# The last feed-forward of a two-layer backbone as seven-product tiles, with sums of weight halves made by accumulating transfers

## The chip, the cores and the metric

The kernel runs on one core of one Trainium2 chip. The metric is the device time of one execution in microseconds (us). The work is shared by TensorE (PE, with its weight loads as PEld), VectorE (DVE), ScalarE (ACT), GpSimd (POOL) and SyncE (SP), which issues the loads.

## The reference

Two layers work on 512 latent tokens and 256 context tokens of width 1024. Each layer is a half-step SwiGLU feed-forward, a mixing of three head groups (grouped-query attention, a gated short convolution, a low-rank attention), and a second half-step feed-forward. Each sub-layer's input is normed and modulated.

```
def rms_norm(x, g):
    y = xf * lax.rsqrt(jnp.mean(xf * xf, axis=-1, keepdims=True) + EPS)
def modulate(h, shift, scale):
    return h * (1 + scale) + shift
def swiglu(h, wg, wu, wd):
    return (jax.nn.silu(h @ wg) * (h @ wu)) @ wd
def half_ffn(h, g, shift, scale, gate, wg, wu, wd):
    return h + 0.5 * gate * swiglu(modulate(rms_norm(h, g), shift, scale), wg, wu, wd)
```

The hidden width of a feed-forward is 2816, which is 22 tiles of 128. Shift, scale and gate are products of nine 1024 x 1024 blocks per layer with silu(c). The output is the latent stream alone, so the last feed-forward (layer 1, the second one) works on the 512 latent tokens only; the other three work on all 768.

## The kernel before, in words

Everything is kept transposed: features on the 128 partitions, tokens along the free dimension. The residual stream is eight tiles xT0 to xT7. A float32 product is made as three fp32r products: operands are split into a high half (a cast on ACT, tiles wh, s and the like) and a low half (raw minus high on DVE, wl), and hi·hi, hi·lo and lo·hi are summed in PSUM (tiles ps and po). So each weight block is loaded by SP, cast by ACT, subtracted by DVE, and then used by TensorE. Weight blocks of 512 KB use the tag wr, which has two buffers (NWR).

Each engine runs its instructions in program order, which the kernel's text fixes: chain and unchain keep the written order on TensorE, DVE and ACT. Every engine call goes through one helper (line 66), so most rows of the profile carry L66 and are told apart by tile names.

`ffn` computes a feed-forward in chunks of hidden tiles. For each hidden tile it makes the gate and the up product, SiLU and their product; after a chunk, a down pass multiplies the chunk's activations by the down weights for the eight outputs and adds gate times the result to xT. A *classical* tile makes both products with full width: 8 k-blocks x 3 products x 2 (gate, up), 48 matmuls of 512 columns when only the latents are there. The three joint feed-forwards (768 tokens) do their first chunk or two like this and then use *seven-product tiles* (class Tile): the tokens and the model width are halved, and seven products of sums of halves replace eight products of halves. The sums of the hidden state are made once (`sums`, `sums_late`); the sums of the weights are made per tile (class Weights: u up weights, g gate weights, s sums). A tile's products p1, p2, p6, p5, p7, p3, p4 are 12 matmuls each, of 384 columns with 768 tokens. While TensorE computes tile m, SP loads the gate and up weights of m+1, DVE forms the sums and ACT and DVE split the four parts: gate (w1), sum (w2), up (w3) and the fourth sum (w4). The joint chunks have three such tiles, then the down pass. The last feed-forward was classical throughout, in chunks of 8, 7 and 7.

`residual` is the last down pass of a sub-layer. It also computes the next sub-layer's norm: squares of xT are summed by products with ones, mean and rsqrt follow on DVE (tiles m), and the result is spread by transposes (R1 for the second token stream). E holds the next sub-layer's first weights; the third pair is split within its loop over k. `pump` does pieces of modulation in between: a piece loads 512 KB (tag mr) and DVE multiplies and sums it by scalar_tensor_tensor into junk, once for latents and once for context. The number npump says how many pieces follow each output; `pump(upto=...)` finishes what a gate needs.

`mixing` projects, norms and attends. Before the attention's units, the norm of the low-rank q (cq) and of k, v (ckv) are counted by products with ones (count_steps), and `uq` makes the q up projections. `wn_late` brings natural-layout weights one k block at a time.

Of the kernel before, what the change touches and what calls it, by code (L numbers as in the profile page):

```python
# [24 lines left out]
CHUNKS = ((0, 8), (8, 7), (15, 7))  # L25
# [17 lines left out]
LATE = {k: 1 for k in range(8)}  # L43
# [4 lines left out]
def tile_net(ctx: ExitStack, tc: tile.TileContext, a, out):  # L48
# [373 lines left out]
    def residual(blocks, rhs, gate, streams, nxt, pre=None, late={}, view=nv, npump=0, ntail=3):  # L422
# [3 lines left out]
        g = mod[gate]  # L426
# [90 lines left out]
        run(4)  # L517
# [27 lines left out]

        for k in range(KD + 1):
# [51 lines left out]
    def ffn(l, f, hin, streams, nxt, pre, npump, late={}):  # L598
# [5 lines left out]
        fast = w == T  # L604
        view = tv if fast else nv
        res = None

        def classical(m, ahead):
# [14 lines left out]
            else:  # L623
                pts = [ps(), ps()]
                for j in range(2):
                    project(full(pts[j]) if fast else plain(pts[j], cols), wgu[j], h)
                parts = [(banks(pts[0]), banks(pts[1]), pairs) if fast else
# [20 lines left out]
        if not fast:  # L648
            for ci, (m0, n) in enumerate(CHUNKS):
                acts = []  # L650
                for m in range(m0, m0 + n):
                    acts.append(classical(m, {}))
                    if m < 18:
                        pump(npump)
                if ci == 0:
                    pump(upto=gate)
                lastc = ci == len(CHUNKS) - 1
                if lastc:
                    before_last()
                res = residual(down(m0, n), acts, gate, streams, nxt if lastc else None, pre, late if lastc else {})  # L660
            return res


        nslow = 2 if i == 0 else 1
        U, V, t1 = [None] * 4, [None] * 2, [None] * 2

        def sums(j):

            X, Y = temp(), temp()
            lo, hi = slice(0, HALF), slice(HALF, T)  # L670
            c = slice(HALF * (j % 2), HALF * (j % 2) + HALF)
            if j % 2 == 0:
                t1[j // 2] = slot()
                V[j // 2] = slot(F32R), slot(F32R)
            T1, (vh, vl) = t1[j // 2][:, c], V[j // 2]
            ve.tensor_add(X, f32(h[j][0]), f32(h[j][1]))
            ve.tensor_add(Y, f32(h[j + 4][0]), f32(h[j + 4][1]))
            ve.tensor_sub(T1, X[:, hi], X[:, lo])
            ve.tensor_sub(X[:, lo], Y[:, hi], X[:, hi])
            ve.tensor_sub(Y[:, hi], Y[:, hi], T1)  # L680
            ve.tensor_sub(Y[:, lo], Y[:, lo], Y[:, hi])
            se.copy(vh[:, c], X[:, lo])
            ve.tensor_sub(vl[:, c], X[:, lo], f32(vh)[:, c])
            U[j] = slot(F32R), slot(F32R)
            se.copy(U[j][0], Y)
            ve.tensor_sub(U[j][1], Y, f32(U[j][0]))

        def sums_late():

            hi = slice(HALF, T)  # L690
            for j in range(4):
                T1 = t1[j // 2][:, HALF * (j % 2):HALF * (j % 2) + HALF]
                se.copy(h[j][0][:, hi], T1)
                ve.tensor_sub(h[j][1][:, hi], T1, f32(h[j][0])[:, hi])

        chunks = FIRST if i == 0 else FAST
        sums_at = (2, 3, 4, 5) if i == 0 else (0, 1, 2)
        for ci in range(nslow):
# [16 lines left out]
            residual(down(m0, n), acts, gate, streams, None, view=tv)  # L715
        W = {}

        class Weights:


            def __init__(self, m):
                self.m = m

# [21 lines left out]
            def fourth(self):  # L745
                ve.tensor_sub(self.g[:, 512:1024], self.g[:, 512:1024], self.s[:, 512:1024])
# [4 lines left out]
            def split_fourth(self):  # L751
                t = pool.tile([P, 1024], F32R, name=nm("w4"), tag="mr", bufs=2)
# [4 lines left out]
        b11 = [tuple(t[:, 0:HALF] for t in h[k]) for k in range(4)]  # L757
        s1 = [tuple(t[:, HALF:T] for t in h[k]) for k in range(4)]
        b21 = [tuple(t[:, 0:HALF] for t in h[k + 4]) for k in range(4)]
        b22 = [tuple(t[:, HALF:T] for t in h[k + 4]) for k in range(4)]  # L760

        def seventh(out, wb, at, mv, new, end=True):

            wh, wl = wb
            for k in range(4):
                c = slice(at + k * P, at + (k + 1) * P)
                for p, (st, m) in enumerate(((wh, mv[k][0]), (wh, mv[k][1]), (wl, mv[k][0]))):
                    te.matmul(out=out[:, 0:HALF], lhsT=st[:, c], rhs=m, start=new and k == 0 and p == 0,
                              stop=k == 3 and p == 2, skip_group_check=True)

        lo, hi = slice(0, HALF), slice(HALF, T)
# [1217 lines left out]
```

## Time and profile before

| | us |
|---|---|
| median of 3 runs | 2800.01 (2799.33 to 2801.71) |
| the profiled execution's own time | 2797.64 |
| its span | 2795.8 |
| TensorE busy | 2696.0 (96%) |
| VectorE busy | 1944.1 (70%) |
| ScalarE busy | 1089.0 (39%) |
| GpSimd busy | 146.9 (5%) |

The shares are means over the whole span. A timeline row gives the start, the length, the engine, the line, the operation with its output, its input and its shape, and in brackets how long the engine stood idle before it and what ended that. The last feed-forward runs from 2421 us to the end.

### The profile page before, as it was taken

What the parts mean: (1) busy time and instruction counts of PE and PEld (TensorE: products, weight loads), DVE (VectorE), ACT (ScalarE), POOL (GpSimd) and SP (SyncE); (2) the same over time, 40 slices, a digit from 0 to 9 for tenths busy, and PEclk for the clock granted to TensorE, in tenths of its full rate; (3) what the DMA queues carried; (4) which work ended last, traced back from release to release, by engine and by line L of the source; (5) the groups of instructions that cost most, each with busy time, mean ns of one, the idle gap of its engine ahead of it and who ended that gap; (6) DMA issues with size and microseconds to landing.
All of it is one profiled execution on the core that took longest, in us unless ns stands there. A gap on an engine that the chain in (4) does not pass through costs nothing. (4 is left out here: it accounts for less than half of the span.)

```text
span 2795.8 us, 38908 instructions
## 1 busy us (share of the span) xinstructions
PE 2696.0 (96%) x15440; PEld 2515.6 (90%) x15440; DVE 1944.1 (70%) x3293; ACT 1089.0 (39%) x1860; POOL 146.9 (5%) x194
## 2 busy tenths in 40 slices
PE   8999999999889998999999999999999999999999
PEld 5999999988788888999999899999988788888887
DVE  6857777777688866777777777777766798633333
ACT  5223333341478532333334333333342477322221
POOL 0000000001132200000000000000000233000000
PEclk9999999999999999999999999999999999999999
DMA  7313333233000321333333133333225101232332
GB/s 245 121 56 103 106 106 106 83 103 115 29 2 9 106 77 53 98 106 107 107 107 102 50 94 107 109 107 108 86 64 172 32 9 56 90 104 91 91 98 91
DMA packets 95269, 251.80 MB, mean 90 GB/s; under 512 B 11376, under 2 KB 40816, under 8 KB 95088
## 3 DMA queue, kind: packets, MB, share of 16 engines
q1 hardware_dynamic: 95088, 249.33, 28.2%
q8 instruction: 121, 1.98, 0.3%
q14 instruction: 60, 0.49, 0.1%
HBM read 247.19 MB, written 2.10 MB: 89 GB/s over the span
## 5 line engine op out<-in xcount | busy, mean ns | idle before, releaser
L66 PE MATMUL ps<-s,wh 128*128 128x384 f32 (+2 forms) x4724 | 1146.5, 349 | 17.3 <-DVE xT L66 11.9
L66 PEld LDWEIGHTS ps<-s,wh 128*128 128x128 f32 x4724 | 832.7, 188 | 90.2 <-issue 15.1
L66 PE MATMUL ps<-s,wl 128*128 128x384 f32 (+2 forms) x2362 | 707.4, 347 | 0.3 <-DVE wl L66 0.3
L66 PE MATMUL po<-s,wh 128*128 128x384 f32 (+2 forms) x2476 | 643.7, 341 | 2.4 <-ACT t L66 1.7
L66 PEld LDWEIGHTS po<-s,wh 128*128 128x128 f32 x2476 | 447.0, 188 | 15.6 <-ACT t L66 2.7
L66 PEld LDWEIGHTS ps<-s,wl 128*128 128x128 f32 x2362 | 428.7, 188 | 32.7 <-DVE wl L66 0.8
L66 PE MATMUL po<-s,wl 128*128 128x384 f32 (+2 forms) x1238 | 422.2, 341 | 0.3 <-DVE wl L66 0.3
L66 ACT CAST wh<-wr 128x1024 fp32r<-128x1024 f32 (+5 forms) x219 | 209.1, 957 | 449.1 <-PE ps L66 319.1
L66 DVE TENSOR_TENSOR wl<-wr,wh 128x1024 fp32r<-128x1024 f32 (+5 forms) x219 | 243.3, 1113 | 194.1 <-ACT wh L66 191.8
L66 DVE SCALAR_TENSOR_TENSOR xT<-ps,mod,xT 128x256 f32<-128x256 f32 (+1 forms) x392 | 212.6, 585 | 193.8 <-PE ps L66 191.9
L66 DVE SCALAR_TENSOR_TENSOR junk<-mr,sb 128x1024 fp8e4<-128x1024 f32 x224 | 273.4, 1221 | 16.4 <-DMA mr<-in_wm_dram 15.5
L66 PEld LDWEIGHTS po<-s,wl 128*128 128x128 f32 x1238 | 232.2, 188 | 6.7 <-DVE wl L66 0.5
L66 PE MATMUL po<-s,s 128*128 128x256 f32 (+3 forms) x952 | 157.6, 316 | 9.6 <-DVE t L66 3.7
L66 PEld LDWEIGHTS po<-s,s 128*128 128x128 f32 x952 | 140.5, 190 | 17.7 <-ACT s L66 6.5
L66 ACT COPY t<-po 128x384 f32<-128x384 f32 (+1 forms) x161 | 76.9, 478 | 195.2 <-PE po L66 194.2
L66 ACT ACTIVATE t<-t 128x384 f32<-128x384 f32 x106 | 55.7, 526 | 238.2 <-DVE t L66 238.2
L66 DVE TENSOR_TENSOR t<-ps,t 128x384 f32<-128x384 f32 (+3 forms) x91 | 55.3, 608 | 112.3 <-PE ps L66 110.3
L66 DVE TENSOR_TENSOR s<-t,s 128x768 fp32r<-128x768 f32 (+2 forms) x129 | 98.6, 767 | 41.0 <-ACT s L66 40.8
L66 ACT CAST s<-t 128x768 fp32r<-128x768 f32 (+2 forms) x129 | 87.9, 684 | 97.2 <-DVE t L66 96.9
L66 PE MATMUL po<-s,w 128*128 128x384 f32 x636 | 119.7, 336 | 0.0
L66 PE MATMUL po<-ident,t 128*128 128x128 f32 x684 | 101.7, 280 | 13.9 <-ACT t L66 12.9
L66 DVE TENSOR_TENSOR t<-po,t 128x384 f32<-128x384 f32 (+2 forms) x169 | 94.0, 557 | 28.6 <-ACT t L66 28.0
(180 smaller groups left out, 3094.6 us busy)
## 6 DMA issues: line engine op xcount, KB each, us to landing
mr<-in_wm_dram SPq DMA_DIRECT2D x128, 512.0 KB, 3.7
wr<-in_wg_dram SPq DMA_DIRECT2D x88, 512.0 KB, 3.5
wu<-in_wu_dram SPq DMA_DIRECT2D x53, 512.0 KB, 3.6
t<-in_wd_dram SPq DMA_DIRECT2D x56, 384.0 KB, 3.4
wr<-in_wu_dram SPq DMA_DIRECT2D x35, 512.0 KB, 3.5
wr<-in_wiT_dram SPq DMA_DIRECT2D x22, 512.0 KB, 3.5
wr<-in_wd_dram SPq DMA_DIRECT2D x16, 512.0 KB, 3.5
wr<-in_wo_dram SPq DMA_DIRECT2D x14, 512.0 KB, 4.0
```

The source lines that it names most:

```text
L66: f(*args, **kw)
```

## The change

The diff makes five changes.

1. *Last feed-forward.* Four classical tiles, then 18 seven-product tiles in chunks of six (LAST), with 256 columns per product. The class Weights gets a second way: SP loads u, and POOL issues three more transfers, a copy of u's first half into s (L751), u's second half added to it (L752), and the gate's first half added onto u (L753). DVE makes one sum of 512 columns (s + g). The fourth sum is an accumulating transfer too (L783: s added onto g's second half). To make all of them additions, the up part is computed negative, and the gate factor `minus` is the negated one. Weights are fetched two tiles ahead. Down weights come one output at a time.
2. *residual.* The third pair of E is split at k 4 and 5 instead of 6; the second stream's counts, mean and rsqrt come one step earlier, ahead of the products.
3. *wn_late.* Two k blocks per load, four loads of 768 columns for eight of 384.
4. *mixing, before the attention.* The rsqrt of ckv stands behind the query splits, a dummy Exp makes ACT load its table earlier, and the counts of cq go from the first up projection into the second, their mean into attention unit 1.
5. *mixing's residual.* npump is 2 instead of 1.

The core of the diff:

```
+LAST = ((0, 4), (4, 6), (10, 6), (16, 6))
-LATE = {k: 1 for k in range(8)}
+LATE = {0: 1, 2: 1, 4: 1, 6: 1}
...
-        run(4)
+        run(8 if ntail == 6 else 4)
...
-            if k == 6 and len(E) == 2:
-                E.append(wsplit(raws[2], 1024))
+            if k == 4 and len(E) == 2:
+                third.extend(pool.tile([P, 1024], F32R, name=nm(t), tag=t, bufs=3) for t in ("wh", "wl"))
+                se.copy(third[0], raws[2])
             if prev is not None:
                 prev.low()
-                if k <= hold or k == KD:
-                    products(k - 1)
-            prev = cur
+            if k == 5 and third:
+                ve.tensor_sub(third[1], raws[2], f32(third[0]))
+                E.append(tuple(third))
             second_update()
             second_square()
             run(3)
-            if k == 2:
+            if k == 1:
                 S[1].zero()
                 S[1].count(S[1].acc, False)
-            if k >= 2:
-                for _ in range(2 if k < 7 else len(s1)):
+            if k >= 1:
+                for _ in range(2 if k < 6 else len(s1)):
...
-            if k == 7:
-
+            if k == 6:
                 S[1].mean()
                 r1 = rsqrt(S[1].ms, S[1].w // P)
+            if prev is not None and (k <= hold or k == KD):
+                products(k - 1)
+            prev = cur
+            if k == 7:
+
                 R1 = po()
...
             def __init__(self, m):
                 self.m = m
+                if not joint:
+
+                    self.u = pool.tile([P, 1024], F32, name=nm("wu"), tag=("mscr", "mq")[m % 2], bufs=1)
+                    self.s = pool.tile([P, 1024], F32, name=nm("ws"), tag="mr", bufs=2)
+                    g, u, lo, hi = a["wg"][i, m], a["wu"][i, m], slice(0, 512), slice(512, 1024)
+                    nc.sync.dma_start(out=self.u, in_=u)
+                    pe.dma_start(out=self.s[:, lo], in_=u[:, lo])
+                    pe.dma_start(out=self.s[:, lo], in_=u[:, hi], accum_op=ALU.add)
+                    pe.dma_start(out=self.u[:, lo], in_=g[:, lo], accum_op=ALU.add)
...
             def sums(self):
                 g, u = self.g, self.u
                 lo, hi = slice(0, 512), slice(512, 1024)
+                if not joint:
+                    ve.tensor_add(self.s[:, hi], self.s[:, lo], g[:, lo])
+                    return
...
             def fourth(self):
+                if not joint:
+                    pe.dma_start(out=self.g[:, 512:1024], in_=self.s[:, 512:1024], accum_op=ALU.add)
+                    return
...
             def split_fourth(self):
+                if not joint:
+                    self.w4 = slot(F32R)[:, 0:512], slot(F32R)[:, 0:512]
+                    se.copy(self.w4[0], self.g[:, 512:1024])
+                    ve.tensor_sub(self.w4[1], self.g[:, 512:1024], f32(self.w4[0]))
+                    return
...
+        def further(m):
+            if not joint and m < NFF:
+                fetch(m)
...
         def update(o, pt):
+            if not joint:
+                x = tv(xT[o], LAT)
+                ve.scalar_tensor_tensor(out=x, in0=cv(pt, LAT), scalar=minus[:, o:o + 1], in1=x, op0=ALU.mult, op1=ALU.add)
+                return
...
                     t.gate1()
+                    further(m + 2)
                     nx.split_gate()
...
-            elif i == 4:
-                rr["ckv"] = rsqrt(stats["ckv"].ms, NT)
...
         stats["cq"].accumulate()
+        se.activation(out=small(1), in_=zeros[:, 0:1], func=AF.Exp)
+        rr["ckv"] = rsqrt(stats["ckv"].ms, NT)
...
-        sums = uq(0, stats["cq"].count_steps(stats["cq"].acc))
-        stats["cq"].mean()
-        sums()
+        uq(0)()
...
-        up_at(0, uq, 1)
+        up_at(0, lambda t: uq(t, stats["cq"].count_steps(stats["cq"].acc)), 1)
         at(0, "end", lambda: uq(2)())
+        at(1, "b", lambda: stats["cq"].mean())
...
-        return residual(lambda o: first_out[0] if o == 0 else wblock(a["wo"][l, o]), rhs, (l, 5), streams, nxt, pre, npump=1)
+        return residual(lambda o: first_out[0] if o == 0 else wblock(a["wo"][l, o]), rhs, (l, 5), streams, nxt, pre, npump=2)
```

How the rows move on the engines. In the names, the number tells tiles of one name apart. First the last feed-forward. POOL's order in the changed kernel, two tiles (wu is u, wr is g, ws is s; POOL had no transfers before):

```order
L751 DMA ws_24392<-in_wu_dram 128x512
L752 DMA ws_24392<-in_wu_dram 128x512
L753 DMA wu_24391<-in_wg_dram 128x512
L783 DMA wr_24361<-ws_24295 128x512
L751 DMA ws_24521<-in_wu_dram 128x512
L752 DMA ws_24521<-in_wu_dram 128x512
L753 DMA wu_24520<-in_wg_dram 128x512
L783 DMA wr_24489<-ws_24392 128x512
```

Each tile is three transfers for the tile two ahead and one onto the gate buffer of the next tile, in one queue.

ACT in the last feed-forward, before (two weight blocks wh per classical tile, SiLU and the activation's split):

```order
L66 CAST wh_24279<-wr_24277 128x1024
L66 CAST wh_24285<-wr_24283 128x1024
L66 CAST wh_24348<-wr_24346 128x1024
L66 CAST wh_24354<-wr_24352 128x1024
L66 ACTIVATE t_24339<-ps_24289 128x512
L66 CAST wh_24417<-wr_24415 128x1024
L66 CAST s_24342<-t_24339 128x512
```

and one tile of the changed kernel (t are gate and up parts from PSUM, wr the gate, ws the sum, wu the up part, s_23606 the fourth part, s_23631 the activation):

```order
L66 COPY t_23483<-po_23484 128x256
L66 ACTIVATE t_23483<-t_23483 128x256
L66 COPY t_23483<-po_23484 128x256
L66 CAST wh_23556<-wr_23505 128x1024
L66 COPY t_23585<-po_23484 128x256
L66 CAST wh_23588<-ws_23408 128x1024
L66 ACTIVATE t_23358<-t_23358 128x256
L66 CAST s_23606<-wr_23377 128x512
L66 CAST wh_23627<-wu_23407 128x1024
L66 CAST s_23631<-t_23358 128x512
```

There are ten rows to a tile instead of four; the split of the gate just loaded (wr_23505) and of its sum (ws_23408) stands ahead of the split of the fourth part out of the gate buffer of the tile at work (wr_23377).

Second, TensorE before the attention of layer 1. Before (ident are transposes, ones the counts of cq, we the first up projection):

```order
L66 MATMUL po_19970<-ident,s_19244 128x128
L66 MATMUL po_19975<-ident,s_19558 128x128
L66 MATMUL po_19975<-ident,s_19595 128x128
L66 MATMUL po_20005<-zeros,ident 128x8
L66 MATMUL po_20005<-ones,s_19849 128x2
L66 MATMUL ps_20004<-we_19938,s_19845 128x288
L66 MATMUL ps_20004<-we_19939,s_19845 128x288
L66 MATMUL ps_20004<-we_19938,s_19846 128x288
```

and the changed kernel at the same place, and some rows on:

```order
L66 MATMUL po_19941<-ident,s_19534 128x128
L66 MATMUL po_19941<-ident,s_19571 128x128
L66 MATMUL ps_19982<-we_19914,s_19821 128x288
L66 MATMUL ps_19982<-we_19915,s_19821 128x288
L66 MATMUL ps_19982<-we_19914,s_19822 128x288
L66 MATMUL ps_19982<-we_19914,s_19880 128x288
```

```order
L66 MATMUL ps_19982<-wh_19920,s_19945 128x288
L66 MATMUL ps_20007<-k_19948,s_19952 128x512
L66 MATMUL ps_20007<-k_19949,s_19952 128x512
L66 MATMUL ps_20007<-k_19948,s_19952 128x256
L66 MATMUL ps_20007<-k_19949,s_19952 128x256
L66 MATMUL po_20019<-zeros,ident 128x8
L66 MATMUL po_20019<-ones,s_19825 128x2
```

The counts stand behind the first up projection and the first scores (k) now.

Third, DVE in the first down pass of layer 0's second feed-forward (junk is modulation, xT the update by the product). Before:

```order
L66 SCALAR_TENSOR_TENSOR junk,mod_8_1_9223<-mr_10223,sb_97 128x1024
L66 TENSOR_TENSOR s_10216<-t_10203,s_10215 128x768
L66 SCALAR_TENSOR_TENSOR junk,mod_8_0_9222<-mr_10223,sb_87 128x1024
L66 TENSOR_TENSOR wl_10320<-wr_10317,wh_10319 128x384
L66 SCALAR_TENSOR_TENSOR junk,mod_8_1_9223<-mr_10227,sb_97 128x1024
L66 TENSOR_TENSOR wl_10347<-wr_10344,wh_10346 128x384
L66 SCALAR_TENSOR_TENSOR junk,mod_8_0_9222<-mr_10227,sb_87 128x1024
L66 TENSOR_TENSOR mod_8_1_9223<-mod_8_1_9223,bm_145 128x8
L66 TENSOR_TENSOR s_10204<-t_10455 128x384
L66 TENSOR_SCALAR mod_8_1_9223<-mod_8_1_9223 128x8
```

and the changed kernel at the same pass:

```order
L66 TENSOR_TENSOR t_10207<-ps_10110,t_10207 128x768
L66 TENSOR_TENSOR wl_10289<-wr_10286,wh_10288 128x384
L66 TENSOR_TENSOR s_10211<-t_10207,s_10210 128x768
L66 TENSOR_TENSOR s_10216<-t_10214 128x384
L66 TENSOR_TENSOR s_10216<-t_10451 128x384
L66 TENSOR_TENSOR t_10214<-t_10215,t_10214 128x384
L66 SCALAR_TENSOR_TENSOR xT_73<-ps_10231,mod_8_0_9208,xT_73 128x2x256
L66 TENSOR_TENSOR t_10215<-t_10215,s_10216 128x384
```

The junk rows are gone from here; they stand in the residual of mixing.

More of the change, by code (lines that the diff above doesn't have):

```diff
@@ L603, in ffn, with whole @@
         w = cols.stop
-        fast = w == T
-        view = tv if fast else nv
-        res = None
+        joint = w == T
+        view = tv if joint else nv
+        hw = w // 2
+        def whole(pt):
+            return full(pt) if joint else plain(pt, cols)
         def classical(m, ahead):
@@ L625, in classical @@
                 for j in range(2):
-                    project(full(pts[j]) if fast else plain(pts[j], cols), wgu[j], h)
-                parts = [(banks(pts[0]), banks(pts[1]), pairs) if fast else
+                    project(whole(pts[j]), wgu[j], h)
+                parts = [(banks(pts[0]), banks(pts[1]), pairs) if joint else
                          (pts[0][:, cols], pts[1][:, cols], lambda t: t[:, cols])]
@@ L647, in ffn @@
         gate = (l, 6 * f + 2)
[L648 to L661, printed above, removed]
@@ L688, in sums_late @@
+            for (th, tl), src in ((t3[j], X[:, lo]),) + (() if joint else ((t4[j], Y[:, lo]), (t2[j], Y[:, hi]))):
+                se.copy(th, src)
+                ve.tensor_sub(tl, src, f32(th))
+            if joint:
+                se.copy(U[j][0], Y)
+                ve.tensor_sub(U[j][1], Y, f32(U[j][0]))
         def sums_late():
-            hi = slice(HALF, T)
+            hi = slice(hw, w)
             for j in range(4):
-                T1 = t1[j // 2][:, HALF * (j % 2):HALF * (j % 2) + HALF]
+                T1 = t1[j // 2][:, hw * (j % 2):hw * (j % 2) + hw]
@@ L714, in ffn @@
                 pump(upto=gate)
-            residual(down(m0, n), acts, gate, streams, None, view=tv)
+            residual(down(m0, n), acts, gate, streams, None, view=view)
         W = {}
+        minus = None
+        if not joint:
+            minus = small(KD)
+            ve.tensor_scalar_mul(minus, mod[gate][0], -1.0)
         class Weights:
```

163 lines of the change are left out of this document (107 added, 56 removed).

## Prediction

> **What bounds the kernel now.** I read the page's busy shares first, then the windows of the last feed-forward and of the places where TensorE waits, then the chain of waits, then single rows. From the page, busy time of each engine and its share of the span:
>
> ```profile
> span 2795.8 us, 38908 instructions
> PE 2696.0 (96%) x15440; PEld 2515.6 (90%) x15440; DVE 1944.1 (70%) x3293; ACT 1089.0 (39%) x1860; POOL 146.9 (5%) x194
> ```
>
> Windows (from:to, then PE, PEld, DVE, ACT and POOL busy with counts, the granted clock, the DMA engines' share, GB/s):
>
> ```profile
> 945.00:987.00 42.00, 42.00 (x237) 36.40 (x236) 33.22 (x54) 11.71 (x17) 0.00 (x0) 1.00 0.42 138
> 1080.00:1100.00 20.00, 13.48 (x68) 13.51 (x69) 15.59 (x34) 3.40 (x6) 0.00 (x0) 0.75 0.19 57
> 2205.00:2219.00 14.00, 12.98 (x65) 11.98 (x66) 6.07 (x17) 6.00 (x9) 0.00 (x0) 0.71 0.01 1
> 1908.00:1952.00 44.00, 43.96 (x255) 43.67 (x253) 31.85 (x49) 17.30 (x26) 0.00 (x0) 1.00 0.36 120
> 2500.00:2600.00 100.00, 100.00 (x430) 80.60 (x429) 35.36 (x44) 24.17 (x28) 0.00 (x0) 1.00 0.31 94
> 2600.00:2700.00 100.00, 100.00 (x431) 80.55 (x430) 36.44 (x47) 25.09 (x30) 0.00 (x0) 1.00 0.31 93
> ```
>
> In the last feed-forward TensorE never stops, while VectorE and ScalarE are busy a third and a quarter of the time. So this stage is as long as its matmuls. The two rows of the chain that matter (start, length, engine, output, count) give the price of one matmul of 256 and of 512 columns:
>
> ```profile
> 2395.32 8.16 PE po L66 x72
> 2443.87 347.48 PE ps L66 x1488
> ```
>
> That is 8.16/72 = 0.1133 us for 256 columns and 347.48/1488 = 0.2335 us for 512. Elsewhere TensorE stands still in few places. First the groups of its waits (total, times, longest), then five of the single waits:
>
> ```profile
> PE po L66 <- DVE m L66: 9.2, 6, 1.9
> PE ps L66 <- DVE xT L66: 11.9, 4, 10.3
> 731.77 0.60 PE L66 MATMUL po<-zeros,ident 128*128 128x12 f32 x2 [2.71 <-DVE k L66]
> 734.14 0.59 PE L66 MATMUL po<-ones,s 128*128 128x2 f32 x2 [1.76 <-DVE s L66]
> 1086.52 1.62 PE L66 MATMUL ps<-s,wh 128*128 128x384 f32 x4 [10.25 <-DVE xT L66]
> 2104.43 1.94 PE L66 MATMUL po<-s,s 128*128 128x384 f32 x5 [3.66 <-DVE t L66]
> 2205.52 0.59 PE L66 MATMUL po<-ones,s 128*128 128x2 f32 x2 [4.79 <-DVE s L66]
> ```
>
> The windows from 1080 and 2205 show the second price of such a wait: the granted clock is 0.75 and 0.71 there, so the matmuls behind the wait run slowly too.
>
> **The last feed-forward, TensorE.** Four of the 22 tiles stay classical. Each of the other 18 took 48 matmuls of 512 columns and now takes seven products of 12, 84 matmuls of 256. Before: 18 x 48 x 0.2335 = 201.7 us. After: 18 x 84 x 0.1133 = 171.3 us by the row at 2395, or 176.5 us if 256 columns cost half of 512 there (0.1168, the stage's own pace). The gain is 30.4 or 25.2; I take 0.115 for one and so 28. A tile is then 84 x 0.115 = 9.7 us of TensorE. The down products are 528 matmuls of 512 in both.
>
> **The last feed-forward, the weights.** What must be done for a tile in those 9.7 us is the same kind of work that the joint feed-forward shows, where it has 14.7 us. This is one such tile; ACT casts a high half, DVE subtracts for the low half:
>
> ```profile
> 1927.65 0.33 SPq L195 DMA_DIRECT2D wr<-in_wg_dram  x1
> 1932.81 1.05 ACT L66 CAST wh<-wr 128x1024 fp32r<-128x1024 f32 x1
> 1933.89 1.23 DVE L66 TENSOR_TENSOR wl<-wr,wh 128x1024 fp32r<-128x1024 f32 x1 [2.46 <-ACT wh L66]
> 1935.04 0.69 DVE L66 TENSOR_TENSOR ws<-wu 128x512 f32<-128x512 f32 x1
> 1936.97 1.05 ACT L66 CAST wh<-ws 128x1024 fp32r<-128x1024 f32 x1
> 1938.06 1.23 DVE L66 TENSOR_TENSOR wl<-ws,wh 128x1024 fp32r<-128x1024 f32 x1 [0.39 <-ACT wh L66]
> 1939.20 0.55 DVE L66 TENSOR_TENSOR t<-po,t 128x384 f32<-128x384 f32 x1
> 1940.21 0.60 ACT L66 CAST w<-wr 128x512 fp32r<-128x512 f32 x1
> 1940.85 0.69 DVE L66 TENSOR_TENSOR w<-wr,w 128x512 fp32r<-128x512 f32 x1 [1.10 <-ACT w L66]
> 1941.57 0.33 SPq L195 DMA_DIRECT2D wr<-in_wg_dram  x1
> ```
>
> The last row is the point: the gate weights have two buffers (wr), and the next gate load starts only when the fourth split of the tile before (w) has left its buffer. That split stands in ACT's and DVE's order behind the splits of the gate that was just loaded. So there is a ring: load, split gate, sum, split sum, gate2, split fourth, load. Its length does not depend on how fast TensorE is. The loads and the two 256-column steps in it have these rows (issue to landing at the end of a DMA row; then count, busy, mean ns):
>
> ```profile
> mr<-in_wm_dram SPq DMA_DIRECT2D x4, 512.0 KB, 4.4
> wr<-in_wg_dram SPq DMA_DIRECT2D x88, 512.0 KB, 3.5
> mr<-in_wm_dram SPq DMA_DIRECT2D x6, 512.0 KB, 4.5
> wr<-in_wd_dram SPq DMA_DIRECT2D x8, 256.0 KB, 2.7
> s<-in_wm_dram SPq DMA_DIRECT2D x8, 256.0 KB, 7.2
> L66 DVE TENSOR_TENSOR s<-s,t 128x256 f32<-128x256 f32 x24 | 9.8, 420 | 0.6
> L66 ACT ACTIVATE t<-xT 128x256 f32<-128x256 f32 x49 | 19.1, 411 | 40.1 <-DVE xT L66 32.7 <-DVE m L66 7.3
> ```
>
> On the engines: cast 1.08 (start to DVE's start), low half 1.15, sum 0.69, cast 1.09, low half 1.14, gate2's addition 0.42, its SiLU 0.41, fourth cast 0.60, its low half 0.69: 7.3 us. The load lands after 3.5 us when little else moves, and after 4.4 to 4.5 in stretches that move 230 to 270 GB/s (the rows with x4 and x6, from windows at 940 and 2100). A new tile moves 0.5 MB of gate, 0.5 of up and four sums of 0.25, about 2 MB in 10 us, so 200 GB/s and more; I take 4.2. The ring is then 11.5 us against 9.7, and each tile inside it loses 1.8. Of the six tiles of a chunk the first finds its weights prepared during the down products and the last prepares none for a neighbour, so 14 of the 18 pay in full: 25 us. With 3.5 it is 14 x 1.1 = 15, with 4.7 it is 14 x 2.3 = 32. So the ring takes back about what TensorE gains: 28 - 25 = 3 us faster.
>
> **The same stage, POOL's transfers.** Three sums leave VectorE (it keeps one of 0.69) for accumulating transfers that POOL issues, four per tile: copy of an up half (L751), addition of the other (L752), addition of the gate half onto up (L753), and the fourth sum (L783). Before has no transfer from POOL at all: its queues are hardware_dynamic and instruction fetch. POOL works in order. The addition (L752) waits for the landing of the copy, and the copy of two tiles on waits for the landing of the fourth sum, which reads its buffer (two buffers, tag mr). That is a second ring: two landings and four issues. By the nearest rows from below, 256 KB land in 2.7 us and an issue takes SP 0.33: 2 x (0.33 + 2.7) + 0.66 = 6.7 us, hidden. By the slowest row of that size, 7.2: 2 x 7.53 + 0.66 = 15.7 us, far above 9.7. These additions touch each element twice, so I take the price of 512 KB under load, 4.5: 2 x 4.83 + 0.66 = 10.3, just hidden behind the first ring's 11.5. The other end goes into the rivals.
>
> By the Trainium skill, DMA: Bandwidth & Descriptors, "Anatomy of one DMA — SWDGE (gpsimd) path", such a transfer takes about 2.0 us plus its bytes over 436e3; for 256 KB that is an estimate of 2.6 us, and the sum would be unchanged. Against the change speaks another rule, SBUF — State Buffer, "Who interferes with whom": GpSimd writes its descriptors through a port pair that VectorE can hold for a whole copy, cast or tensor_scalar in a two-port mode. VectorE's rows in a tile above are all TENSOR_TENSOR, so by that rule nothing is held; no run here shows it.
>
> **Other edits to this stage.** The sums of the hidden state (four calls in the classical tiles) and the update by one STT per output lie on VectorE, which is busy 36 us in 100 there; the gain `minus` is one tiny op. I take 0, at worst 3 us.
>
> **The modulation moved (npump 2).** Behind the wait of 10.25 us stood these two rows and four like them, in the way of the xT update that TensorE waited for:
>
> ```profile
> 1072.97 1.22 DVE L66 SCALAR_TENSOR_TENSOR junk<-mr,sb 128x1024 fp8e4<-128x1024 f32 x1
> 1074.12 0.08 DVE L66 DVE_READ_ACCUMULATOR junk<-mr,sb 128x1 f32 x1
> ```
>
> The step to the next row is 1.15 us, six of them 6.9 us, so about 3.3 of the wait stay and with the shorter wait 1 us of slow clock goes. The rows go to the mixing residual, where VectorE was busy 33.2 of 42 us: ten more are 11.5, spread over six outputs of 8.4 us, which it barely holds; I set 2 us against it (0 to 6). Net 6 faster.
>
> **The attention start.** The count of the q norm, for which TensorE waited 4.79 us in layer 1 and 1.76 in layer 0, stands behind the first up projection now, whose inputs are there; the rsqrt of ckv, which ran before k, stands behind the k work (2.71). The table load (1.28 us) comes early:
>
> ```profile
> 2213.88 1.28 ACT L66 ACT_TABLE_LOAD   x1
> ```
>
> The waits sum to 9.3; a clock of 0.71 over 14 us is up to 4 more in one layer. The next limit is the k and query split that scores need, which ends within 0.8 us of the old wait's end, so part of the wait returns behind 18 matmuls. I take 12 for both layers, 5 to 15 as bounds.
>
> **Residuals and late weights.** Six waits on the norm's m (9.2 us) go away for the second stream, since its mean is made a step earlier; the third split comes two steps earlier, with 2 us of waits of its own. I take 9, 3 to 11. wn_late's batching and the earlier norm shorten the 3.66 at 2104: 3, 0 to 4.
>
> **Sum.** 3 + 6 + 12 + 9 + 3 = 33 us faster. The profiled execution is 2797.6 us and the median of the three runs 2.4 above it: 2797.6 - 33 + 2.4 = **2767 us**.
>
> **The rivals.** (1) *No ring loss:* loads land early enough, or gate2 and the splits overlap better than in a chain. For it: before's joint tiles lose nothing (43.96 of 44 us at 1908); against it: they have 5 us more each. 28 + 30 = 58 faster, 2742. (2) *Half of the waits come back:* another operand is late where one wait goes, as with k behind the q count; and loads take 4.7. 28 - 32 + 15 = 11 faster, 2789. (3) *POOL's ring binds:* place L751 to L783, price 15.7 us a tile, so 14 x 6.0 = 84 lost, 28 + 30 - 84 = 26 slower, 2826. It decides from 58/14 = 4.1 us of loss a tile on, a ring of 13.8 us, which is a landing of 6.2 us. For it: no row of such a transfer exists, four of them wait in one queue, and 7.2 occurs when many loads are under way; against it: 2.7 in ordinary stretches. (4) *The change doesn't do what it says* is hardly one: the order of TensorE has 708 rows more, 18 x 36 = 648 of them these products.
>
> **How the numbers follow.** Forecast 0.45, own range 2752 to 2780; (1) 0.20; (2) 0.20; (3) 0.15. For this kernel 0.2%, 5.6 us, is about what can be told from no change. (2) and (3) each reach into that band a little, 0.05 in all, and (3) keeps 0.15 above it: faster 0.80, same 0.05, slower 0.15. The range reaches to (1) and (2) and a part of (3): 2738 to 2806.
>
> **What would show it.** Right: in the last feed-forward windows of 100 us with TensorE at 80 to 90% and waits on wh or wl in the middle of chunks, gate loads about 11.5 us apart, POOL's issues not the ones waited for; at 1086 a wait of 3 us; no wait over 2 us at the attention starts. Wrong: TensorE full in those windows (rival 1); tiles 13 us or more apart with SP or DVE waiting on DMA from POOL (rival 3); new waits of the old length on k, s or t (rival 2).

## The result, and the profile after

The changed kernel takes 2767.7 us (median; 2763.6 to 2771.8) where the kernel before takes 2799.7 on the same chips: a ratio of 0.9884, 95% interval 0.9866 to 0.9903, 32 us faster. The forecast was 2767. The profile shows that the sum came out right from two terms that were both wrong. The page of the changed kernel:

```profile
span 2768.6 us, 40713 instructions
PE 2675.8 (97%) x16088; PEld 2530.8 (91%) x16088; DVE 2028.9 (73%) x3463; ACT 1144.9 (41%) x1989; POOL 204.5 (7%) x266
q0 software_dynamic: 9216, 18.88, 3.6%
```

TensorE is busy 20 us less, and POOL has a queue of its own. The windows below are cut at the same updates of xT in both kernels (columns as in the prediction): from before layer 0's mixing to its second feed-forward, layer 1's mixing, and the last feed-forward. First before, then after:

```profile
560.00:1100.00 540.00, 492.98 (x3107) 449.07 (x3107) 402.50 (x772) 261.94 (x529) 79.43 (x98) 0.97 0.19 62
2060.00:2415.40 355.40, 330.75 (x2103) 298.08 (x2101) 268.61 (x531) 193.60 (x389) 66.73 (x90) 0.98 0.21 70
2415.40:2796.00 380.60, 371.55 (x1687) 302.96 (x1686) 139.01 (x195) 98.68 (x126) 0.00 (x0) 1.00 0.30 92
```

```profile
560.00:1076.00 516.00, 487.68 (x3102) 445.54 (x3101) 407.14 (x775) 261.50 (x526) 78.77 (x98) 0.98 0.20 67
2035.00:2376.50 341.50, 326.98 (x2108) 295.25 (x2107) 265.26 (x523) 193.06 (x386) 66.75 (x90) 1.00 0.21 69
2376.50:2768.60 392.10, 358.50 (x2328) 322.95 (x2326) 223.58 (x373) 154.97 (x261) 58.31 (x72) 0.98 0.52 137
```

The two mixing stages are 24.0 and 13.9 us shorter: TensorE's idle time falls by 18.7 and 10.1, and the same matmuls (but for a few records) take 5.3 and 3.8 less, at a mean granted clock of 0.98 and 1.00 where it was 0.97 and 0.98. By the end of the last mixing the changed kernel is 38.9 us ahead. The last feed-forward then gives 11.5 of them back: it was busy 371.55 of 380.6 us and is busy 358.50 of 392.1. TensorE's gain of 13 us in busy time is outweighed by 24.5 us more of idle time (9.1 before, 33.6 after).

The waits of TensorE after (total, times, longest) show the same exchange. The 10.25 us wait for xT, and nearly all of the 9.2 us for m, are gone, and a wait for ACT's copies out of PSUM has come; the second fence is the last feed-forward alone, from 2440 us on:

```profile
PE po L66 <- ACT t L66: 39.6, 35, 2.9
PE ps L66 <- DVE xT L66: 2.2, 3, 1.2
PE po L66 <- DVE t L66: 1.5, 1, 1.5
PE po L66 <- DVE m L66: 1.1, 2, 0.9
```

```profile
PE po L66 <- ACT t L66: 24.0, 16, 2.9
```

The chain of waits after runs through the ring that the prediction described, row for row, for one tile (start, length, what):

```profile
2695.76 4.37 DMA wr<-in_wg_dram
2700.16 0.04 issue
2700.20 1.06 ACT wh L66
2701.28 1.23 DVE wl L66
2702.51 0.61 DVE ws L66
2703.15 0.04 issue
2703.19 1.06 ACT wh L66
2704.31 1.11 issue
2705.42 0.43 DVE t L66
2705.97 0.22 issue
2706.20 0.61 ACT s L66
2706.83 0.07 DVE s L66
2706.90 0.54 issue
2707.44 0.11 DVE t L66
2707.55 4.81 DMA wr<-in_wg_dram
```

Load, gate split, sum, sum's split, gate2, fourth split, load: 2707.55 - 2695.76 = 11.8 us, where 11.5 was forecast. But POOL's rows show a second ring in the same tile:

```profile
2692.01 1.58 POOL L783 DMA_DIRECT2D wr<-ws  x1
2698.81 0.57 POOL L751 DMA_DIRECT2D ws<-in_wu_dram  x1 [5.22 <-DVE t L66]
2703.41 0.90 POOL L752 DMA_DIRECT2D ws<-in_wu_dram  x1 [4.03 <-issue]
2703.95 1.27 POOL L753 DMA_DIRECT2D wu<-in_wg_dram  x1
2704.49 1.64 POOL L783 DMA_DIRECT2D wr<-ws  x1
```

From one fourth sum (L783) to the next are 12.5 us: 6.8 from its issue to that of the first copy, 4.6 from there to the addition, which waits for the copy's landing, and 1.1 more. What the copy waits for has two names in the profile: DVE's t in this row, the fourth sum's landing in five others (total, times, longest):

```profile
POOL ws L751 <- DMA wr<-ws: 23.1, 5, 5.1
```

The transfers from POOL land late (KB each, median us, from a window over the chunks):

```profile
ws<-in_wu_dram POOLq DMA_DIRECT2D x32, 256.0 KB, 3.7
wu<-in_wg_dram POOLq DMA_DIRECT2D x16, 256.0 KB, 5.3
wr<-ws POOLq DMA_DIRECT2D x17, 256.0 KB, 5.9
wr<-in_wg_dram SPq DMA_DIRECT2D x16, 512.0 KB, 4.6
```

Each takes longer than the 2.7 us of a plain 256 KB load before, and the fourth sum longer than the 4.5 that the prediction took. So there are two rings of nearly one length, both above TensorE's pace. One tile doesn't say more: over the three chunks the gate loads are 11.0 to 12.9 us apart (12.1 in the mean) and the fourth sums 10.6 to 13.6 (11.7). Which ring holds the tiles the trace alone can't say. Times on different chips differ by some 0.2%, so what follows compares ratios to the kernel before on the same chip, and stage lengths inside the profiles.

### The profile page after: what moved, and what is told of

It reads as the page before. It is cut to its first block, busy times and chain, and to the rows that moved or that the text cites. A ratio compares the mean times of both kernels' runs of the same rounds, so it can differ in the third digit from the quotient of the medians.

```text
span 2768.6 us, 40713 instructions
## 1 busy us (share of the span) xinstructions
PE 2675.8 (97%) x16088; PEld 2530.8 (91%) x16088; DVE 2028.9 (73%) x3463; ACT 1144.9 (41%) x1989; POOL 204.5 (7%) x266
## 5 line engine op out<-in xcount | busy, mean ns | idle before, releaser
L66 PE MATMUL ps<-s,wh 128*128 128x384 f32 (+2 forms) x4292 | 988.7, 339 | 7.9 <-ACT t L66 4.1
L66 PE MATMUL po<-s,wh 128*128 128x384 f32 (+2 forms) x3196 | 779.5, 330 | 26.4 <-ACT t L66 25.7
L66 PE MATMUL ps<-s,wl 128*128 128x384 f32 (+2 forms) x2146 | 612.9, 338 | 0.7 <-DVE wl L66 0.5
L66 PEld LDWEIGHTS po<-s,wh 128*128 128x128 f32 x3196 | 563.0, 190 | 43.8 <-ACT t L66 29.9
L66 PE MATMUL po<-s,wl 128*128 128x384 f32 (+2 forms) x1598 | 525.9, 329 | 0.0
L66 DVE TENSOR_TENSOR wl<-wr,wh 128x1024 fp32r<-128x1024 f32 (+4 forms) x195 | 209.8, 1078 | 159.1 <-ACT wh L66 158.9
L66 DVE SCALAR_TENSOR_TENSOR junk<-mr,sb 128x1024 fp8e4<-128x1024 f32 x224 | 273.2, 1220 | 13.4 <-DMA mr<-in_wm_dram 12.6
L66 ACT CAST wh<-wr 128x1024 fp32r<-128x1024 f32 (+4 forms) x195 | 179.6, 925 | 232.3 <-PE ps L66 143.0
L66 ACT COPY t<-po 128x384 f32<-128x384 f32 (+2 forms) x215 | 96.9, 451 | 218.0 <-PE po L66 216.3
L66 PEld LDWEIGHTS po<-s,s 128*128 128x128 f32 x1168 | 166.6, 189 | 11.8 <-DVE pl L66 2.5
L1370 POOL TENSOR_TENSOR t<-s 128x544 f32<-128x544 f32 (+1 forms) x12 | 12.3, 1037 | 1861.4 <-ACT s L66 1855.4
L66 ACT CAST s<-t 128x768 fp32r<-128x768 f32 (+3 forms) x144 | 93.0, 650 | 107.5 <-DVE t L66 105.5
L66 DVE TENSOR_TENSOR s<-t,s 128x768 fp32r<-128x768 f32 (+3 forms) x144 | 104.0, 726 | 45.1 <-ACT s L66 44.6
```

Source lines behind the costliest of these rows:

```text
L66: f(*args, **kw)
L1370: pe.tensor_mul(sq[:, lo:544], x[:, lo:544], x[:, lo:544])
```

## Experiments: the two halves

*sides_only* has all edits but the last feed-forward; *last_only* has the new last feed-forward alone.

```
 sides_only, against the change:  function ffn and CHUNKS of the kernel before
 last_only, against before:       function ffn and LAST of the change, and
-        g = mod[gate]
+        g = mod[gate] if isinstance(gate, tuple) else gate
```

> The change without its last feed-forward (classical tiles in chunks of 8, 7 and 7 as before); the other four edits stay. By the milestones of the two traces, the updates of xT run 38.9 us earlier by the end of the last mixing, and the last feed-forward then gives 11.7 us back. If that is right: 2800 - 39 = 2761 us, 6 to 7 us faster than the whole change. If the seven-product tiles gain 3 us, as the prediction had it, the edits here are worth only 30: 2770 us.

Measured: 2755.6 us, ratio 0.9836 (0.9811 to 0.9860), 46 us faster than before (39 to 53). The 39 of the milestones is at the edge of that, the 30 of the prediction outside.

> The new last feed-forward alone, everything else as before. If the milestones are right and the parts add: 2800 + 12 = 2812 us. If it gains 3 us as predicted: 2797. If it were the source of the gain: 2768.

Measured: 2817.7 us, ratio 1.0051 (1.0033 to 1.0070), 14 us slower than before, where the milestones said 12. The halves add up: 0.9836 + 0.0051 = 0.9887 against 0.9884. The seven-product last feed-forward, as it stands, costs time, and the change would have been faster without its largest part.

## Experiments: which ring holds the tiles

*early4* moves one split in the order: the fourth part of the tile at work ahead of the gate just loaded.

```
                 t.take2()
+                if not joint and not end:
+                    t.w.split_fourth()
                 if nx:
                     nx.split_gate()
...
                 p.gate2()
-                if not end:
+                if joint and not end:
                     t.w.split_fourth()
```

> The change with one thing moved: the split of the fourth part stands ahead of the split of the gate just loaded, in the order of ACT and DVE, so the gate buffer is free some 6 us earlier and the load no longer closes a ring of one tile. Theory of the gate ring: the stage loses little in its chunks, about 25 to 35 us of the 39 lost there come back: 2735 to 2743 us. Rival, POOL's ring (two landings and four issues, 12.5 us in one tile of the trace): the tiles stay about 12.5 us apart, and the time stays within 5 us of 2768 or gets worse.

*dve1* leaves the order of the splits and takes two of POOL's four transfers away: DVE adds the two halves of the up weights. That addition, and with it POOL's remaining transfer for the tile two ahead (the gate half onto up), stands at the end of the tile now, behind the fourth sum.

```
-                    pe.dma_start(out=self.s[:, lo], in_=u[:, lo])
-                    pe.dma_start(out=self.s[:, lo], in_=u[:, hi], accum_op=ALU.add)
+                    ve.tensor_add(self.s[:, lo], u[:, lo], u[:, hi])
```

> The change with the first weight sum made by DVE (two POOL transfers per tile for four), the split of the fourth part left where it was. Theory of two rings of nearly the same length (gate 11.8, POOL 12.5 us a tile): opening POOL's alone leaves the gate ring, which is a little shorter with less traffic: 11.0 to 11.5 us a tile, a ratio of 0.984 to 0.987 against 0.9884. If POOL's ring alone were the bound: 0.980, as with both open. If the gate ring alone: 0.988.

*early4_dve1* does both.

> As the run before, and the first sum (both halves of the up weights) is made by one DVE addition of 512 columns instead of two transfers of POOL; POOL keeps two transfers per tile. Gate ring alone: no more than the run before, perhaps 1 to 3 us worse, as DVE has 0.69 us more per tile. POOL's ring: here both rings are open, tiles come at TensorE's pace of 9.7 to 9.9 us, 2768 - 35 = 2733 us, and clearly faster than the run before.

Measured: early4 0.9845 (0.9823 to 0.9867), dve1 0.9817 (0.9799 to 0.9834), early4_dve1 0.9803 (0.9774 to 0.9832), against 0.9884 for the change. The three chunks (from their first 256-column product to the first down product) say it without the scatter of whole runs; the sum rows of windows over them, in the order change, early4, dve1, early4_dve1:

```profile
sum 208.70, PE 184.71 PEld 181.22 DVE 121.44 ACT 100.43 POOL 49.68; mean PE 61.57 PEld 60.41 DVE 40.48 ACT 33.48 POOL 16.56
```

```profile
sum 197.50, PE 181.30 PEld 178.22 DVE 123.69 ACT 98.72 POOL 48.02; mean PE 60.43 PEld 59.41 DVE 41.23 ACT 32.91 POOL 16.01
```

```profile
sum 195.40, PE 178.55 PEld 175.04 DVE 130.67 ACT 99.56 POOL 25.01; mean PE 59.52 PEld 58.35 DVE 43.56 ACT 33.19 POOL 8.34
```

```profile
sum 188.00, PE 178.27 PEld 174.95 DVE 132.04 ACT 98.41 POOL 25.08; mean PE 59.42 PEld 58.32 DVE 44.01 ACT 32.80 POOL 8.36
```

Opening the gate's ring alone gains 11.2 us, less than the 25 to 35 of its theory and more than the 5 of POOL's. Opening POOL's alone gains 13.3. Both gain 20.7. So neither ring was the one bound: each stood close behind the other, and both expectations for early4 were wrong. Not all of these gains need be the rings': the granted clock is 0.98, 0.95 and 0.95 in the chunks of the change, 1.00, 1.00 and 0.95 in those of early4 (its third takes 68.1 us, the others 64.9 and 64.5), and 1.00 in the other two kernels.

In dve1 the fourth sum lands after 3.3 us instead of 5.9. Two transfers of POOL fewer are under way there, but that this is the cause is not shown: the transfer onto up, left in the same queue, still takes 5.4.

```profile
wr<-ws POOLq DMA_DIRECT2D x18, 256.0 KB, 3.3
```

The spacing of the tiles gives the length of each ring where it is alone. In dve1 the gate loads come 11.3 us apart, within the 11.0 to 11.5 expected of the gate's ring, though the ratio is below the 0.984 to 0.987 that went with it. In early4 the fourth sums of POOL's ring come 11.3 us apart in the mean. So neither is longer by what the runs show, and with both closed the tiles are further apart (11.7 to 12.1) than with either. If they were independent, opening the shorter would gain nothing; they seem to lengthen each other, but how is not shown.

With both open the tiles were expected at TensorE's pace of 9.7 to 9.9 us; they came 10.7 us apart, with TensorE waiting at each tile for a copy out of PSUM by ACT:

```profile
2574.72 0.50 PE L66 MATMUL po<-s,wh 128*128 128x256 f32 x2 [0.51 <-ACT t L66]
2585.41 0.51 PE L66 MATMUL po<-s,wh 128*128 128x256 f32 x2 [0.65 <-ACT t L66]
```

*early4_dve3* asks whether POOL has a part in that: all sums on DVE, no transfer from POOL.

```
-                    pe.dma_start(out=u[:, lo], in_=g[:, lo], accum_op=ALU.add)
+                    ve.tensor_add(u[:, lo], g[:, lo], u[:, lo])
...
-                    pe.dma_start(out=self.g[:, 512:1024], in_=self.s[:, 512:1024], accum_op=ALU.add)
+                    ve.tensor_add(self.g[:, 512:1024], self.g[:, 512:1024], self.s[:, 512:1024])
```

> As early4_dve1 with all sums of weight halves on DVE, nothing from POOL: DVE has 1.4 us more per tile than there (two additions of 512 columns), a good 9 of 9.8 us. If transfers from POOL still held the tiles at 10.7 us, this would be faster than 0.9803. If the ring of ACT and DVE holds them, the two additions lengthen it by 1.2 us: 12.0 us a tile, 14 x 1.2 = 17 us slower, a ratio of 0.986.

Measured: 0.9836 (0.9817 to 0.9855), and in the chunks:

```profile
sum 195.00, PE 181.03 PEld 175.61 DVE 149.89 ACT 98.01 POOL 0.00; mean PE 60.34 PEld 58.54 DVE 49.96 ACT 32.67 POOL 0.00
```

This is 7 us longer than early4_dve1, and the tiles are 11.3 us apart instead of 10.7: the direction of a ring of ACT and DVE, but half of the 1.2 us a tile of the sum. By itself the run can't exclude a small part of POOL, as it has both fewer transfers and longer work of DVE. rings_open below speaks against it: it keeps POOL's two transfers, and its tiles come 9.97 us apart.

*early4_dve1_take1* and *rings_open* look for that ring's place. The first puts take1 ahead of two casts on ACT, the second also puts the first gating behind the gate's split.

```
                 t.p1()
                 p.act1()
+                if not joint:
+                    t.take1()
                 t.w.split_up()
...
(rings_open also)
                 t.p6()
-                t.gate1()
+                if joint:
+                    t.gate1()
                 further(m + 2)
...
                     nx.split_gate()
+                if not joint:
+                    t.gate1()
```

> As early4_dve1, and ACT copies the first product out of PSUM (take1) ahead of the casts of the up part and of the activation, not behind them. In early4_dve1 gate loads are 10.7 us apart with TensorE waiting 0.5 to 0.9 us per tile on that copy, and no DMA in the ring. Theory: what is left there is a ring of ACT and DVE from copy to copy; two casts (1.04 and 0.5) leave it, it becomes shorter than TensorE's 9.6 to 9.8, and 14 tiles gain 0.6 to 0.9 us each: a ratio of 0.976 to 0.978 against 0.9803. Rival: DVE's and ACT's own work or the loads hold the 10.7, and the copy is only what ends last: no change within 2 us.

Measured: 0.9795 (0.9777 to 0.9813), no difference from early4_dve1 that can be told, and the tiles still 10.7 us apart (the chunks take 187.2 us); only the copy that TensorE waits for is the next one. The rival held: the copy was what ended last. The sum row of the chunks, and ACT's rows, which show what take2 stands behind, a SiLU that waits 1.77 us for DVE's addition:

```profile
sum 187.20, PE 179.23 PEld 175.71 DVE 131.80 ACT 98.46 POOL 25.02; mean PE 59.74 PEld 58.57 DVE 43.93 ACT 32.82 POOL 8.34
```

```profile
2584.93 0.42 ACT L66 ACTIVATE t<-t 128x256 f32<-128x256 f32 x1 [1.77 <-DVE t L66]
2585.25 0.35 ACT L66 COPY t<-po 128x256 f32<-128x256 f32 x1
2585.50 0.62 ACT L66 CAST s<-wr 128x512 fp32r<-128x512 f32 x1
```

> As early4_dve1_take1, and the first gating (an addition on DVE, a SiLU on ACT) stands behind the fourth and the gate split, not ahead of ACT's second copy out of PSUM (take2). In early4_dve1_take1 that copy is what TensorE waits for, 0.85 us a tile: it stands behind a SiLU that waits for DVE. Theory: the last ring is ACT and DVE handing to each other through that SiLU (10.7 us a tile); without it the tiles run at TensorE's 84 x 0.117 = 9.8, so 14 x 0.85 = 12 us: a ratio of 0.975 to 0.976 against 0.9795. Rival: another pair of handovers is as long (two idle times of DVE of 0.8 and 0.5 us a tile remain): 0.979.

Measured: 2740.0 us, 0.9797 (0.9780 to 0.9814). In the chunks:

```profile
sum 180.40, PE 174.94 PEld 171.82 DVE 132.94 ACT 98.89 POOL 25.03; mean PE 58.31 PEld 57.27 DVE 44.31 ACT 32.96 POOL 8.34
```

Once a chunk is under way, the tiles are 9.97 us apart now. The chunks take 6.8 us less than in early4_dve1_take1, from which only the first gating's place differs, and 7.6 less than in early4_dve1; TensorE's waits for copies over the three chunks fall from 9.7 us to 4.6 (early4_dve1, then rings_open):

```profile
PE po L66 <- ACT t L66: 9.7, 14, 1.7
```

```profile
PE po L66 <- ACT t L66: 4.6, 4, 2.0
```

The whole run's ratio doesn't show this: it is that of early4_dve1 within the intervals of some 5 us, and by the number alone the rival's 0.979 fits and the theory's 0.975 to 0.976 does not. Of the 7.6 us the down passes between the chunks lose 2.6 again, so that from the first 256-column product to the end of the profile 5.0 are left (295.3 for 300.3). So the handover through the SiLU was the ring in the stage; that it makes the kernel faster is not shown.

## Experiments: what the other edits gave

Three kernels undo one edit of sides_only each, and one makes one edit alone.

```
(sides_npump1, against sides_only)
-        return residual(... streams, nxt, pre, npump=2)
+        return residual(... streams, nxt, pre, npump=1)
(sides_no_attn, against sides_only)
+            elif i == 4:
+                rr["ckv"] = rsqrt(stats["ckv"].ms, NT)
...
-        se.activation(out=small(1), in_=zeros[:, 0:1], func=AF.Exp)
-        rr["ckv"] = rsqrt(stats["ckv"].ms, NT)
...
-        uq(0)()
+        sums = uq(0, stats["cq"].count_steps(stats["cq"].acc))
+        stats["cq"].mean()
+        sums()
...
(sides_no_resid, against sides_only)
-        run(8 if ntail == 6 else 4)
+        run(4)
...
-            if k == 4 and len(E) == 2:
+            if k == 6 and len(E) == 2:
+                E.append(wsplit(raws[2], 1024))
...
-            if k == 6:
+            if k == 7:
                 S[1].mean()
...
(resid_only, against before: the same lines the other way round)
```

The milestones in the expectations are the times of the same xT update in two traces.

> The kernel sides_only (all of the change but the last feed-forward) with one piece of modulation per output of the mixing's residual, as before. By the milestones the lead grows from 9.8 to 23.1 us at the first down pass behind it, so the loss should be 12 to 13 us against sides_only: a ratio of 0.988 against 0.9836. By the prediction's term it would be 6 us: 0.9857.

Measured: 0.9866 (0.9851 to 0.9881), 8 us back against 0.9836. Both ratios have intervals, so this is 8 give or take 8, and excludes neither the 6 nor the 12 to 13.

> The kernel sides_only with the work ahead of both attentions as before (rsqrt of ckv early, no early table load, counts and mean of cq in the first up projection). By the milestones the lead grows by 8.3 us over layer 0's attention and by 11.5 over layer 1's, so it should lose about 20 us: a ratio of 0.9907. By the prediction's term 12: 0.988. If late weights (wn_late) or the residual made those steps, it loses less than 10.

Measured: 0.9871 (0.9857 to 0.9886), 10 us back, give or take 8: the prediction's 12 fits, the milestones' 20 does not.

> The kernel sides_only with the residual's order as before (third split at k 6, second stream's mean at k 7). By the milestones this edit gains 1 to 3 us at each of five places, 7 to 9 in all: a ratio of 0.9865 against 0.9836. The prediction's term was 9 us. If the waits only move elsewhere, less than 4: 0.985 or below.

Measured: 0.9921 (0.9899 to 0.9944), 24 us back, give or take 9, more than twice what either theory had.

> The kernel before with the residual's new order alone (third split at k 4 and 5, second stream's counts and mean a step earlier). Undoing it in sides_only cost 24 us by the ratios, though the waits that came back sum to 12.6 us (1.18 + 1.92 + 0.98 + 1.53 + 1.92 + 1.92 + 1.50 + 1.67). If the waits are all there is: 12 to 13 us faster, a ratio of 0.9955. If the order gains more than its waits (slow clock behind them, work moved along): 20 us or more, 0.993. By the prediction's term, 9 us: 0.9968.

Measured: 0.9938 (0.9925 to 0.9952), 18 us faster than before, give or take 4. The waits alone were 12.6, which is 0.9955, just outside. Single waits of TensorE in resid_only show one thing more:

```profile
1080.29 1.62 PE L66 MATMUL ps<-s,wh 128*128 128x384 f32 x4 [10.29 <-DVE xT L66]
2094.07 3.22 PE L66 MATMUL po<-s,s 128*128 128x384 f32 x9 [6.94 <-DVE t L66]
```

The wait for xT is whole, as it belongs to npump. The wait at layer 1's first products, 3.66 us before, has grown to 6.94: with the norm earlier, the late weights are later by comparison. With wn_late's pairs it is 1.5 us, in the whole change and in sides_no_resid alike. So 3.3 us of the residual's gain are lost again when it is alone, and not together with wn_late, which no run has alone. The 18 and the 24 differ by less than their intervals, so no more is read from that. Engine rows of the page of sides_only and of sides_no_resid:

```profile
PE 2679.7 (97%) x15440; PEld 2499.7 (91%) x15440; DVE 1945.5 (71%) x3285; ACT 1087.0 (40%) x1854; POOL 146.1 (5%) x194
```

```profile
PE 2692.0 (97%) x15440; PEld 2511.4 (90%) x15440; DVE 1946.0 (70%) x3285; ACT 1087.4 (39%) x1854; POOL 146.8 (5%) x194
```

The profile of sides_no_resid is 27.9 us longer: TensorE is idle 15.6 us more, and the same 15440 matmuls take 12.3 us longer. A slow clock behind the waits that came back would do that, but so would a chip or an execution that runs a little slower throughout. The matmuls part the two: the largest group takes the same time in both (count, busy us, mean ns; sides_only, then sides_no_resid),

```profile
L66 PE MATMUL ps<-s,wh 128*128 128x384 f32 x2720 | 603.2, 337 | 3.8 <-ACT t L66 1.9 <-DVE xT L66 0.9
```

```profile
L66 PE MATMUL ps<-s,wh 128*128 128x384 f32 x2720 | 603.0, 337 | 3.9 <-ACT t L66 1.9 <-DVE xT L66 1.0
```

while 596 of 256 columns take 139.2 us instead of 133.4. Around waits that came back (1510 to 1560, 2030 to 2130 and 2390 to 2420 us) the granted clock is 0.93 to 0.95, and 1.00 at the same places in sides_only. So it is not an execution that is slower throughout, and the slow clock stands where the waits are. It does not follow every wait: before has one of 1.92 us at 593, in a window (565 to 600) with a clock of 1.00.

## Why the prediction was right, and where it was wrong

*The total* was right, and so was its direction, but by two errors of opposite sign: the last feed-forward was to be 3 us faster and is 14 slower, the other edits were to give 30 us and give 46. That the sum is within 1 us of the forecast is luck. Of the signs given, TensorE's 88% in the chunks, the gate loads and the short waits at the attention starts (1.6 us at most) came; but TensorE waits for ACT's copies there, not for wh or wl.

*TensorE's gain* was right as to the pace: rings_open runs its 1488 matmuls of 256 columns in 180.4 us with few waits, and TensorE is busy 174.9 of them, which is 0.1175 each; half of the 512-column row (0.1168) was nearer than the row at 2395. So the gain was at the 25 us end. In the change itself the stage's busy time fell by 13 us only.

*The ring of the gate buffer* was right as a mechanism, row for row, with 11.8 us for 11.5 in the tile shown and 11.3 where dve1 leaves it alone. The step that failed is the one behind it: "the ring takes back about what TensorE gains". The chunks take 208.7 us against 174 at TensorE's pace (1488 matmuls at 0.1168; 24 more stand in the down passes), so they lose some 35 and not 25. Of these, 24.0 are idle time of TensorE; the other 11 are slower matmuls, 184.7 us for 174, at the granted clock of 0.95 to 0.98 given above. The prediction counted a slow clock behind other waits and put it at nothing here. Whether it lengthens the tiles or only fills what the rings leave idle is not shown. The factor 14 is too high as well: by the prediction's own words on the first and the last tile of a chunk, 12 of the 18 tiles pay in full, 22 us.

*POOL's transfers* is the mis-sized term. The prediction took 4.5 us for a landing and 0.33 for an issue, and called a ring of 10.3 us hidden. Measured are 3.7 and 5.9 for the two landings in it and issues of 0.57 to 1.64, a ring of 12.5 in the tile shown, 11.7 in the mean and 11.3 alone. It was the rival (3)'s place with less than its price: below its point of decision of 13.8 us, so the change stayed faster. By the Trainium skill, DMA: Bandwidth & Descriptors, "Anatomy of one DMA — SWDGE (gpsimd) path", the estimate for 256 KB was 2.6 us; POOL's transfers in the change have medians of 3.7 to 5.9 us, and none in the traces landed in less than 2.8; the measurement decides.

*The order behind the rings* was not seen: that ACT's copies out of PSUM stand behind a SiLU that waits for DVE, 10.7 us a tile with both other rings open.

*The edits outside* were 30 in the prediction and are 46 (39 to 53) by sides_only. npump: 6 expected, 8 measured, and no wait for xT is longer than 1.2 us, where 3.3 was to stay. The attention: 12 and 10. The residual is the term that was mis-sized: 9 expected, 18 alone and 24 when undone. Its sum took 9 of 11 us of waits, of which 12.6 came back when it was undone, and put the slow clock behind them at nothing, where matmuls took 12.3 us longer.

*Rival (1)*, no loss in the ring, is what rings_open approaches by another order: 2740.0 us, where 2742 was given. That the numbers meet is luck again: 2742 was 28 from TensorE and 30 from the other edits, and rings_open is only some 11 us ahead of sides_only (0.9797 and 0.9836, with intervals that touch).

## What to carry to other kernels

When a stage with much slack on the other engines is made shorter on TensorE, list each ring that closes within one tile: buffer by buffer, from a load to the split that frees it, and queue by queue. The pace here was set by the rings, not by the busy shares, and behind each ring that was opened the next stood less than 1 us a tile away. Edits of the order alone (split what frees a buffer first, copy out of PSUM ahead of anything that waits for another engine) opened two of the three here, the second by the stage's length only. And when several edits are predicted as a sum, run the halves apart: a total that fits can hide a part that costs time.

The kernel rings_open, at 0.9797 (0.9780 to 0.9814), beats both kernels, the change (0.9866 to 0.9903) clear of the intervals; sides_only (0.9811 to 0.9860), which leaves the last feed-forward as it was, comes close to it.

## What was not expected of the hardware

An accumulating transfer from one part of on-chip memory to another of 256 KB took 5.9 us when four transfers of POOL came per tile and 3.3 when two did, while the 512 KB gate load by SP in the same stretches (the change and dve1) took 4.6 and 3.3, and the up load 4.4 and 5.1. POOL's issues grew from 0.57 us (a plain copy) to 0.9, 1.27 and 1.64 when three accumulating ones followed each other, and stayed at 0.87 when they came singly.
